# The last step of the last token block's second MLP product by whole token tiles, and two products' operands made ahead in the other blocks

## The chip, the cores and the metric

The kernel runs on one core of a Trainium2 chip. Its engines take their instructions in a fixed order each and wait for one another by semaphores: TensorE (PE) for matmuls, VectorE (DVE), ScalarE (ACT), GpSimd (POOL), and the queues of transfers, most of which SyncE (SP) issues. The metric is the time of one launch on the device, in microseconds; of several runs the median counts. Nearly all work in the kernel is in float32.

## The reference

One step of a hybrid decoder layer, on a new prompt of 2,048 tokens and on 64 sample tokens (8 sequences of 8 tokens, with 8,192 cached tokens each). Attention with forgetting and a matrix-memory branch are mixed, projected, added to the input and normalized; then comes the MLP, which the change is about:

```python
x1 = _layer_norm(DN_ALPHA * x + mix, ln1_g, ln1_b)
hid = jnp.square(jax.nn.relu(x1 @ w1))
return _layer_norm(DN_ALPHA * x1 + hid @ w2, ln2_g, ln2_b)
```

`x1` has 1,024 columns, `hid` 4,096. The prompt's rows go to `y_prompt`, the sample's to `y_sample`.

## The kernel before

**Phases.** Earlier phases project the input, attend over the prompt and run the matrix memory. The sample tokens' attention over the cache runs beside everything else: its pieces (`attend`) are put between other work by a pace (`tick`), read cached keys and values by gathers, and go on into the MLP phase. The MLP, `phase_c` (L1262), comes last.

**Blocks and steps.** Tokens stand in tiles of 128, 0 to 15 for the prompt; tile 16 holds the 64 sample tokens. `CB` makes four blocks of them, 0 to 3; the last has 12, 13, 14, 15 and 16 (576 tokens), the others four tiles (512). In each block the 4,096 hidden units are taken in eight steps `p` of 512. `hidden(p, half)` (L1325) makes 256 of them from x1 and `w1` in PSUM tiles `ph`, and ACT squares the positive part into `hq`. `output(p, ...)` (L1412) multiplies the step's 512 hidden units with 512 rows of `w2` and adds into the rows `y`. The loop at the end of the phase does the first half of the next step's hidden units, then this step's output, then the other half.

**Products in three parts.** PE multiplies float32 exactly enough only by halves: an operand is split by ACT into a rounded high part (`split_hi`, L154) and by DVE into the rest (`split_lo`, L157), and `mm3` (L162 to L165) does high x high, high x low and low x high. `hh` and `hl` are the parts of hidden units, `wh` and `wl` those of weights, `x1h` and `x1l` those of x1. The sample tile's output is multiplied without a split, in `two_sides` (L168 to L170), for two halves of the hidden units side by side.

**Strassen's products.** For one step and four tiles, the second product is a 2 x 2 block product: token tiles in two pairs, hidden units in two halves, columns of `w2` in two halves. `output` does it by Strassen's method with seven products in place of eight: sums of hidden blocks are made by DVE in `made` (L1392 is the sum's helper), sums of blocks of weights were made in earlier phases and lie in `dw2`, and each product's PSUM tiles are added to several rows of y by `add` (L1355, its instruction L1362). A product is 12 matmuls of 128x512; a step has 84. The order is 1, 5, 6, 3, 7, 2, 4 in blocks 0 to 2 and 1, 2, 5, 3, 6, 7, 4 in block 3. `operands` and `made` load, sum and split for a product; they run three products ahead of PE in program order, and `ahead(p, ...)` makes the first ones before `output` begins: the first two of the order in steps 0 to 6, product 1 alone in step 7.

**Weights.** In blocks 0 to 2 they are loaded into five buffers `wr` that the first product's weights use too; in block 3 into the six places of a ring (`kT`, `spare`) that the sample attention has left. `wh` and `wl` have four buffers each, `hh` and `hl` three.

**What stands around step 7.** In blocks 0 to 2 step 7 also turns the next block's x1: PE transposes a tile (`px`, L1171), and ACT and DVE split it into `x1h` and `x1l`; the next block's first product needs all of them. In block 2 the hidden stage before step 7 does the sample tokens' output projection and first norm (`sampled`, L1294 to L1316; instructions on L1310, L1311, L1315, and `norm_quick`, L187 to L198), since tile 16 belongs to block 3. `C["normed"]`, the norm's last DVE instruction on L197, is put ahead of everything that `output` of that step issues, by `issue_after`; what `ahead` has made is outside of this.

**The end.** In block 3 `add` counts the additions to each half row (`due`). When a half is complete its statistics are taken (L1370), and when both are, `norm_quick` norms the tile and sends it out: L189 and L191 on DVE, a power on POOL (L192), two instructions each on L195 and L197 on DVE, two transfers (L198).

**Order.** The instructions of each engine are put in a fixed order when the program is built, by a scheduler that follows the dependences and the `issue_after` orders; so an edit can move instructions that it does not name.

Of the kernel before, what the change touches and what calls it, by code (L numbers as in the profile page):

```python
# [52 lines left out]
def body(ctx, tc, I, O, stages):  # L53
# [841 lines left out]
    def phase_b():  # L895
# [173 lines left out]
        for n in range(len(units) + LA):  # L1069
            if 10 <= n < 16 and acc[1] is not None:  # L1070
                attend()
            w2_due[0] += 64 * (n % 8 // 2 + 1) / 130 if n >= 8 else 0
            while n and len(w2_done) < min(64, w2_due[0]):
                w2_sum()
            if n == 60:
                wo.extend(half_wo(0, q) for q in range(4))
            if n < len(units):
                h, g = units[n]
                sc[n] = scores(Z[h], g)
                if h == 0 and g % 2 == 0 and g < 6:  # L1080
                    keys(Z[0], g // 2 + 1)
                if h < 7:
                    if g == 3:
                        Z[h + 1] = head(h + 1)
                        forget_values(Z[h + 1], 0, S)
                    if g >= 4:
                        keys(Z[h + 1], g - 4)
                if n + 1 < len(units):
                    queries(Z[units[n + 1][0]], units[n + 1][1])
            if n >= LA:  # L1090
                h, g = units[n - LA]
                values(Z[h], g, sc.pop(n - LA))
# [183 lines left out]
    def phase_c():  # L1276
# [5 lines left out]
        def vecs(l):  # L1282
            g = bcast(I[f"ln{l}_g"], 0, D, f"g{l}", pcw, tag="wr", bufs=5)
            b = bcast(I[f"ln{l}_b"], 0, D, f"b{l}", pcw, tag="wr", bufs=5)
            return g, b
# [42 lines left out]
        for ci, blk in enumerate(CB):  # L1328
# [28 lines left out]
            def add(t, half, ps, op=OP.add):  # L1357
                n = tok_n(t)
                y = ys[t][:n, half * 512:half * 512 + 512]
                due[t, half] = due.get((t, half), 0) + 1  # L1360
                if (t, half) in seen:
                    V.tensor_tensor(y, y, ps, op=op)  # L1362
                else:
                    seen.add((t, half))
                    V.scalar_tensor_tensor(y, y, ALPHA, ps, op0=OP.mult, op1=op)
                if ci == 3 and due[t, half] == 8 * sums[blk.index(t) // 2, half]:
                    first_ = t not in stats
                    if first_:
                        stats[t] = pc.tile([128, 2, 6], F32, name="ln_s2", bufs=5)
                    V.bn_stats(stats[t][:n, half], y)  # L1370
                    if not first_:
                        norm_quick(ys[t][:n], n, stats.pop(t), *C["gb"], pc, y_out(t))

            def operands(p):

                f1, f2 = H.pop((p, 0)), H.pop((p, 1))
                a11, a21, a12, a22 = f1[:, :, 0:256], f1[:, :, 256:512], f2[:, :, 0:256], f2[:, :, 256:512]
                s = ph.tile([128, 2, 256], F32, name="s", bufs=1)

                def split(x):  # L1380
                    h = ph.tile([128, 2, 256], F32R, name="hh", bufs=3)
                    l = ph.tile([128, 2, 256], F32R, name="hl", bufs=3)
                    split_hi(h, x)
                    split_lo(l, x, h)
                    return h, l

                def w(src):
                    wr = (spare() if W > 512 else raw()).rearrange("p (k c) -> p k c", k=2)
                    SY.dma_start(wr, src.rearrange("p (k c) -> p k c", k=2))
                    return (*piece(None, wr), wr)  # L1390

                v = lambda o, x, y, op: V.tensor_tensor(o, x, y, op=op)  # L1392

                def made(n):
                    if n == 1:
                        r = split(a11), w(I["w2"][p, 0])
                        v(s, a21, a22, OP.subtract)
                        v(a21, a11, a21, OP.subtract)
                        v(a11, s, a11, OP.subtract)
                    elif n == 5:  # L1400
                        r = split(s), w(dw2[p, 0])
                        v(s, a12, a11, OP.add)
                    else:
                        r = {6: lambda: (split(a11), w(dw2[p, 2])), 3: lambda: (split(s), w(I["w2"][p, 3])),
                             7: lambda: (split(a21), w(dw2[p, 1])), 2: lambda: (split(a12), w(I["w2"][p, 2])),
                             4: lambda: (split(a22), w(dw2[p, 3]))}[n]()
                    return r

                hs = [f[:, :, 512:576] for f in (f1, f2)] if W > 512 else []
                return made, hs  # L1410
# [3 lines left out]
            def output(p, ahead, begun=None):  # L1414
# [12 lines left out]
                extra = {2: (1, ((0, 0, ADD), (0, 1, SUB), (1, 0, ADD))), 3: (5, ((0, 1, ADD), (1, 1, ADD)))}  # L1427
                for at_, n in enumerate(order):
                    kind, first_, last_, r0, half, op = plan[n]
                    if p == 7 and at_ == 2 and ci == 3:  # L1430
                        C["gb"] = vecs(2)
                    for m in order[:at_ + 3]:
                        if m not in ops:
                            ops[m] = made(m)
# [26 lines left out]
                if begun:  # L1461
                    for hf in range(2):
                        turn(ci + 1, 4, hf, begun)

            def y_out(t):
                return O["y_sample"].rearrange("b t d -> (b t) d") if t == 16 else O["y_prompt"][0, t * 128:(t + 1) * 128]

# [6 lines left out]
            def ahead(p, *ns):  # L1474
                made, hs = operands(p)
                r = made, hs, {}
                for n in ns:
                    r[2][n] = made(n)
                return r
# [2 lines left out]
            hidden(0, 1)  # L1482
            for p in range(8):
                pre = []
                if p < 7:
                    hidden(p + 1, 0, lambda: pre.append(ahead(p, *order[:2])))
                else:
                    pre.append(ahead(p, 1))
                if p == 6:
                    vx["more"] = None  # L1490
                with ExitStack() as es_:
                    if "normed" in C:
                        es_.enter_context(tc.issue_after(C.pop("normed").ins))
                    output(p, pre[0], begun if p == 7 and ci < 3 else None)
                if p == 7 and ci < 3:
                    vx["more"] = landing
                    C["w1"] = w1_pieces(0)
                    C["gb"] = vecs(2)
                    later = [normed(t, ys[t], C["gb"]) for t in blk]
                if p == 6 and ci < 3:  # L1500
                    take_back()
                    begun = [x1_load(t) for t in CB[ci + 1][:2]]
                if p == 6 and ci == 2:
                    while acc[1] is not None:
                        tick(100.0)
                if p < 7:
                    hidden(p + 1, 1, sampled if p == 6 and ci == 2 else None)
        es.close()

    wo = []  # L1510
# [434 lines left out]
```

## Time and profile before

| what | value |
|---|---|
| median of 3 runs (lowest, highest) | 3236.75 us (3231.51, 3241.11) |
| profiled execution | 3245.35 us |
| its span, first to last instruction | 3242.4 us |
| mean granted clock of PE | 0.987 |
| start of the MLP blocks 0, 1, 2, 3 | 1568.65, 1984.77, 2412.1, 2827.38 us |
| output of step 7 in block 2 | 2780.7 to 2827.4 us |
| output of step 7 in block 3, to the last instruction of DVE | 3195.9 to 3238.87 us |

The profile is of one execution. The page begins with each engine's busy time and its share of the span; a window is a stretch of the span with the same numbers. In a timeline each row has the start, the duration, the engine, the line of the kernel and the operation with the tile that it writes and those that it reads; `x16` says that a row stands for 16 instructions of one kind in a row, and a bracket at the end of a row is the engine's idle time before it and what ended it. A duration includes the part in which the next instruction of the engine has already begun, so prices are read from one start to the next. The view of the waits adds up such idle times by pairs: who waited for whom, in all, how often, and the longest.

### The profile page before, as it was taken

What the parts mean: (1) busy time and instruction counts of PE and PEld (TensorE: products, weight loads), DVE (VectorE), ACT (ScalarE), POOL (GpSimd) and SP (SyncE); (2) the same over time, 40 slices, a digit from 0 to 9 for tenths busy, and PEclk for the clock granted to TensorE, in tenths of its full rate; (3) what the DMA queues carried; (4) which work ended last, traced back from release to release, by engine and by line L of the source; (5) the groups of instructions that cost most, each with busy time, mean ns of one, the idle gap of its engine ahead of it and who ended that gap; (6) DMA issues with size and microseconds to landing.
All of it is one profiled execution on the core that took longest, in us unless ns stands there. A gap on an engine that the chain in (4) does not pass through costs nothing. (4 is left out here: it accounts for less than half of the span.)

```text
span 3242.4 us, 57713 instructions
## 1 busy us (share of the span) xinstructions
PE 3127.7 (96%) x21585; PEld 2535.8 (78%) x21585; DVE 2095.6 (65%) x5062; ACT 1489.0 (46%) x2940; POOL 907.2 (28%) x974
## 2 busy tenths in 40 slices
PE   8899999999989999999999999999999999899997
PEld 8898998998956666677677777776777777698895
DVE  6866657456478788544466568656586665766658
ACT  3342343343378888522344345343454444344442
POOL 0021233323334333276233423433333121000000
PEclk9999999999989999999999999999999999999999
DMA  5465776866667776487887878868779766543322
GB/s 188 128 220 174 254 225 202 277 238 232 228 220 204 185 181 150 171 300 262 294 291 277 296 270 308 317 243 328 289 282 338 279 212 210 208 147 137 121 95 81
DMA packets 339775, 734.34 MB, mean 226 GB/s; under 512 B 63656, under 2 KB 177704, under 8 KB 338600
## 3 DMA queue, kind: packets, MB, share of 16 engines
q1 hardware_dynamic: 252360, 416.18, 39.2%
q0 software_dynamic: 83520, 304.12, 26.7%
q10 hardware_dynamic: 3616, 10.36, 0.9%
q8 instruction: 170, 2.79, 0.3%
q14 instruction: 109, 0.89, 0.1%
HBM read 677.71 MB, written 86.38 MB: 236 GB/s over the span
## 5 line engine op out<-in xcount | busy, mean ns | idle before, releaser
L157 DVE TENSOR_TENSOR wl<-wr,wh 128x1024 fp32r<-128x1024 f32 x300 | 366.0, 1222 | 249.5 <-ACT wh L154 241.9
L163 PE MATMUL ph<-x1h,wh 128*128 128x512 f32 (+1 forms) x1280 | 455.2, 356 | 0.0
L164 PE MATMUL ph<-x1l,wh 128*128 128x512 f32 (+1 forms) x1280 | 453.0, 354 | 0.2 <-DVE x1l L157 0.2
L165 PE MATMUL ph<-x1h,wl 128*128 128x512 f32 (+1 forms) x1280 | 450.5, 354 | 0.7 <-DVE wl L157 0.4
L154 ACT ACTIVATE wh<-wr 128x1024 fp32r<-128x1024 f32 x300 | 315.4, 1053 | 290.1 <-PE ph L164 162.4
L1662 POOL DMA_INDIRECT kT<-cache_k,idxK x256 | 275.8, 1077 | 540.7 <-PE sQ L1685 477.2
L163 PE MATMUL py<-wh,hh 128*128 128x512 f32 x896 | 358.3, 403 | 6.4 <-ACT hh L154 3.7
L164 PE MATMUL py<-wl,hh 128*128 128x512 f32 x896 | 352.4, 395 | 5.5 <-DVE wl L157 5.5
L165 PE MATMUL py<-wh,hl 128*128 128x512 f32 x896 | 349.2, 395 | 2.1 <-DVE hl L157 2.1
L1362 DVE TENSOR_TENSOR y<-y,py 128x512 f32<-128x512 f32 x416 | 281.5, 682 | 98.9 <-PE py L165 94.8
L163 PE MATMUL pm<-xh,whi 128*128 128x256 f32 (+1 forms) x1024 | 299.5, 292 | 0.0
L164 PE MATMUL pm<-xl,whi 128*128 128x256 f32 (+1 forms) x1024 | 295.5, 289 | 0.0
L165 PE MATMUL pm<-xh,wlo 128*128 128x256 f32 (+1 forms) x1024 | 294.5, 288 | 0.0
L1773 POOL DMA_INDIRECT vt<-cache_v,idxV x164 | 177.7, 1084 | 384.3 <-PE sO L1797 316.9
L163 PEld LDWEIGHTS ph<-x1h,wh 128*128 128x128 f32 x1280 | 241.2, 188 | 40.8 <-issue 7.8
L165 PEld LDWEIGHTS ph<-x1h,wl 128*128 128x128 f32 x1280 | 240.3, 188 | 37.1 <-issue 3.7
L164 PEld LDWEIGHTS ph<-x1l,wh 128*128 128x128 f32 x1280 | 241.2, 188 | 34.4 <-issue 3.3
L163 PE MATMUL pm<-whi,xh 128*128 128x256 f32 (+2 forms) x816 | 238.1, 292 | 9.4 <-ACT whi L154 8.4
L164 PE MATMUL pm<-wlo,xh 128*128 128x256 f32 (+2 forms) x816 | 233.8, 287 | 0.6 <-DVE wlo L157 0.6
L165 PE MATMUL pm<-whi,xl 128*128 128x256 f32 (+2 forms) x816 | 233.4, 286 | 0.0
L163 PEld LDWEIGHTS py<-wh,hh 128*128 128x128 f32 x896 | 169.0, 189 | 60.4 <-issue 14.5
L1003 ACT ACTIVATE S<-S,mx 128x512 f32<-128x512 f32 (+2 forms) x320 | 207.7, 652 | 18.4 <-DVE mx L989 17.1
(363 smaller groups left out, 6829.1 us busy)
## 6 DMA issues: line engine op xcount, KB each, us to landing
wr<-w SPq DMA_DIRECT2D x200, 512.0 KB
wra<-w_in SPq DMA_DIRECT2D x104, 512.0 KB
wr<-dw SPq DMA_DIRECT2D x96, 512.0 KB
dw<-w POOLq DMA_DIRECT2D x48, 512.0 KB, 8.1
Rb<-dR SPq DMA_DIRECT2D x128, 128.0 KB
kT<-dw SPq DMA_DIRECT2D x32, 512.0 KB
kT<-w SPq DMA_DIRECT2D x24, 512.0 KB
xn<-xp_t SPq DMA_DIRECT2D x16, 512.0 KB
```

What stands on the lines that cost most here:

```text
L154: last["ACT"] = A.activation(dst, src, AF.Copy, scale=scale)
L157: r = (eng or V).tensor_tensor(dst, src, hi.bitcast(F32), op=OP.subtract)
L163: T.matmul(ps, wh, xh, start=first, stop=False, skip_group_check=shared)
L164: T.matmul(ps, wh, xl, start=False, stop=False, skip_group_check=shared)
L165: last["PE"] = T.matmul(ps, wl, xh, start=False, stop=stop, skip_group_check=shared)
L1003: last["ACT"] = A.activation(sp[:, :w], sp[:, :w], AF.Exp, bias=mx[:, 7:8], accum_out=lp[:, k:k + 1])
L1362: V.tensor_tensor(y, y, ps, op=op)
L1662: G.indirect_dma_start(out=piece(n), out_offset=None, in_=ck, in_offset=IO(ap=idxK[:, b, j // 2, j % 2:j % 2 + 1], axis=0))
L1773: vx["last"] = G.indirect_dma_start(out=vt.rearrange("p f c -> p (f c)"), out_offset=None, in_=cv, in_offset=IO(ap=idxV[:, b, (kt % 4) * 4 ...
```

## The change

In block 3 step 7 is done by a new function, `plain`, without sums: for each of the tiles 12 to 15 and each half of the columns, four pairs of hidden units and weights into one PSUM tile, 12 matmuls, eight such groups, 96 matmuls in all; then one `add`. The weights are four blocks of `w2` itself. Blocks 0 and 2 are loaded and split by `early`, which `hidden(7, 1)` calls between its two halves, 1 and 3 in `plain`. The fourth low half of hidden units uses the buffer of `s`, which is free without sums. `hh` gets a fourth buffer, in all steps. The sample tile's four half sums come from the same eight matmuls of `two_sides`, two to a PSUM tile for one half of the columns. The last addition that starts a row's statistics is counted anew. In step 7 of blocks 0 to 2 `ahead` makes products 1 and 5, not 1 alone.

```diff
--- before.py
+++ after.py
@@ -1070,7 +1070,7 @@
             if 10 <= n < 16 and acc[1] is not None:
                 attend()
             w2_due[0] += 64 * (n % 8 // 2 + 1) / 130 if n >= 8 else 0
-            while n and len(w2_done) < min(64, w2_due[0]):
+            while n and len(w2_done) < min(60 if False else 64, w2_due[0]):
                 w2_sum()
             if n == 60:
                 wo.extend(half_wo(0, q) for q in range(4))
@@ -1363,7 +1363,7 @@
                 else:
                     seen.add((t, half))
                     V.scalar_tensor_tensor(y, y, ALPHA, ps, op0=OP.mult, op1=op)
-                if ci == 3 and due[t, half] == 8 * sums[blk.index(t) // 2, half]:
+                if ci == 3 and due[t, half] == 7 * sums[blk.index(t) // 2, half] + (2 if t == 16 else 1):
                     first_ = t not in stats
                     if first_:
                         stats[t] = pc.tile([128, 2, 6], F32, name="ln_s2", bufs=5)
@@ -1378,7 +1378,7 @@
                 s = ph.tile([128, 2, 256], F32, name="s", bufs=1)
 
                 def split(x):
-                    h = ph.tile([128, 2, 256], F32R, name="hh", bufs=3)
+                    h = ph.tile([128, 2, 256], F32R, name="hh", bufs=4)
                     l = ph.tile([128, 2, 256], F32R, name="hl", bufs=3)
                     split_hi(h, x)
                     split_lo(l, x, h)
@@ -1427,8 +1427,6 @@
                 extra = {2: (1, ((0, 0, ADD), (0, 1, SUB), (1, 0, ADD))), 3: (5, ((0, 1, ADD), (1, 1, ADD)))}
                 for at_, n in enumerate(order):
                     kind, first_, last_, r0, half, op = plan[n]
-                    if p == 7 and at_ == 2 and ci == 3:
-                        C["gb"] = vecs(2)
                     for m in order[:at_ + 3]:
                         if m not in ops:
                             ops[m] = made(m)
@@ -1462,6 +1460,56 @@
                     for hf in range(2):
                         turn(ci + 1, 4, hf, begun)
 
+            def weight(src):
+                wr = spare().rearrange("p (k c) -> p k c", k=2)
+                SY.dma_start(wr, src.rearrange("p (k c) -> p k c", k=2))
+                return (*piece(None, wr), wr)
+
+            lastw = {}
+
+            def plain(p):
+
+                f = H.pop((p, 0)), H.pop((p, 1))
+                C["gb"] = vecs(2)
+                x = {}
+
+                def part(r, n):
+                    h = ph.tile([128, 2, 256], F32R, name="hh", bufs=4)
+                    if len(x) < 3:
+                        l = ph.tile([128, 2, 256], F32R, name="hl", bufs=3)
+                    else:
+                        l = ph.tile([128, 2, 256], F32R, name="hl4", tag="s", bufs=1)
+                    a = f[n][:, :, r * 256:r * 256 + 256]
+                    split_hi(h, a)
+                    split_lo(l, a, h)
+                    x[r, n] = h, l
+
+                for n in range(2):
+                    part(0, n)
+                for q in (1, 3):
+                    lastw[q] = weight(I["w2"][p, q])
+                for n in range(2):
+                    part(1, n)
+                for half in range(2):
+                    ps = ppc.tile([128, 512], F32, name="ph", tag="ph", bufs=2)
+                    for k in range(2):
+                        two_sides(ps, [(f[n][:, k, 512:576], lastw[n * 2 + half][2][:, k]) for n in range(2)], k == 0, k == 1)
+                    for n in range(2):
+                        add(16, half, ps[n * 64:n * 64 + 64])
+                for i in range(4):
+                    r, c = i // 2, slice(i % 2 * 128, i % 2 * 128 + 128)
+                    for half in range(2):
+                        ps = ppc.tile([128, 512], F32, name="py", bufs=4)
+                        for n in range(2):
+                            (h, l), (wh, wl, _) = x[r, n], lastw[n * 2 + half]
+                            for k in range(2):
+                                mm3(ps, h[:, k, c], l[:, k, c], wh[:, k], wl[:, k], n == k == 0, n == k == 1, True)
+                        add(blk[i], half, ps)
+
+            def early():
+                for q in (0, 2):
+                    lastw[q] = weight(I["w2"][7, q])
+
             def y_out(t):
                 return O["y_sample"].rearrange("b t d -> (b t) d") if t == 16 else O["y_prompt"][0, t * 128:(t + 1) * 128]
 
@@ -1482,10 +1530,13 @@
             hidden(0, 1)
             for p in range(8):
                 pre = []
+                if p == 7 and ci == 3:
+                    plain(p)
+                    break
                 if p < 7:
                     hidden(p + 1, 0, lambda: pre.append(ahead(p, *order[:2])))
                 else:
-                    pre.append(ahead(p, 1))
+                    pre.append(ahead(p, *order[:2]))
                 if p == 6:
                     vx["more"] = None
                 with ExitStack() as es_:
@@ -1504,7 +1555,7 @@
                     while acc[1] is not None:
                         tick(100.0)
                 if p < 7:
-                    hidden(p + 1, 1, sampled if p == 6 and ci == 2 else None)
+                    hidden(p + 1, 1, {2: sampled, 3: early}.get(ci) if p == 6 else None)
         es.close()
 
     wo = []
```

The orders below are of the built programs, without times. The numbers tell buffers apart. First DVE in block 2's step 7, from the first sum of hidden blocks: y_30222 is the sample tile, s_30317 a sum that is product 5's operand, wr_30337 product 5's weights, wr_30348 those of product 6. Before:

```order
L1392 TENSOR_TENSOR s_30317<-hq_29890,hq_30188 128x512
L1392 TENSOR_TENSOR hq_29890<-hq_29890 128x2x256
L1392 TENSOR_TENSOR hq_29890<-s_30317,hq_29890 128x2x256
L189 BN_AGGR ln_m2_30279<-ln_s2_30237 64x2
L191 TENSOR_SCALAR ln_r2_30281<-ln_m2_30279 64x1
L195 SCALAR_TENSOR_TENSOR y_30222<-y_30222,ln_m2_30279,g1_30216 64x512 x2
L197 SCALAR_TENSOR_TENSOR y_30222<-y_30222,ln_r2_30281,b1_30218 64x512 x2
L157 TENSOR_TENSOR hl_30334<-s_30317,hh_30333 128x512
L157 TENSOR_TENSOR wl_30340<-wr_30337,wh_30339 128x1024
L157 TENSOR_TENSOR hl_30345<-hq_29890,hh_30344 128x512
L157 TENSOR_TENSOR wl_30351<-wr_30348,wh_30350 128x1024
```

With the change, from the weights of product 5 (here wr_30335), which are split beside the sample attention's own work (L1868) and ahead of the projection (L1310):

```order
L157 TENSOR_TENSOR wl_30338<-wr_30335,wh_30337 128x1024
L1868 TENSOR_REDUCE mixs_2655<-sT_30164 64x8 x8
L1310 SCALAR_TENSOR_TENSOR y_30222<-y_30222,py_30224 64x256
...
L1392 TENSOR_TENSOR s_30317<-hq_29890,hq_30188 128x512
L157 TENSOR_TENSOR hl_30332<-s_30317,hh_30331 128x512
L1392 TENSOR_TENSOR s_30317<-hq_30188,hq_29890 128x512
L195 SCALAR_TENSOR_TENSOR y_30222<-y_30222,ln_m2_30279,g1_30216 64x512 x2
L197 SCALAR_TENSOR_TENSOR y_30222<-y_30222,ln_r2_30281,b1_30218 64x512 x2
L157 TENSOR_TENSOR hl_30345<-hq_29890,hh_30344 128x512
L157 TENSOR_TENSOR wl_30351<-wr_30348,wh_30350 128x1024
```

The low half of product 5's operand (hl_30332) and the third sum now stand ahead of the norm; the weights of product 5 are gone from the stretch; product 6's operand and weights (hl_30345, wl_30351) still follow the norm.

PE with the change, from its leaving the hidden stage of block 3's last step; ph_33925 and ph_33934 are the sample tile's sums for the two halves of the columns, py_33953 is tile 12's first half, py_33969 its second, py_33995 tile 13's first:

```order
L170 MATMUL ph_33925<-kT_11264,hq_33468 64x512
L170 MATMUL ph_33925<-kT_11264,hq_33776 64x512
L163 MATMUL py_33953<-wh_33832,hh_33899 128x512
...
L165 MATMUL py_33953<-wh_33837,hl_33904 128x512
L163 MATMUL py_33969<-wh_33908,hh_33899 128x512
L163 MATMUL py_33995<-wh_33832,hh_33899 128x512
...
L164 MATMUL py_33995<-wl_33833,hh_33899 128x512
L170 MATMUL ph_33934<-kT_11264,hq_33468 64x512
L170 MATMUL ph_33925<-kT_11264,hq_33776 64x512
L170 MATMUL ph_33934<-kT_11264,hq_33776 64x512
L164 MATMUL py_33969<-wl_33909,hh_33899 128x512
```

Where before a whole product of Strassen's came first and the sample tile's eight matmuls in one piece after 24 matmuls, three of the eight now come first and five after 18 matmuls of whole tiles.

DVE at the very end. y_31015 to y_31021 are tiles 12 to 15. Before:

```order
L1370 BN_STATS ln_s2_34097<-y_31019 128x6
L1370 BN_STATS ln_s2_34106<-y_31021 128x6
L1362 TENSOR_TENSOR y_31019<-y_31019,py_33898 128x512
L191 TENSOR_SCALAR ln_r2_34081<-ln_m2_34079 128x1
L195 SCALAR_TENSOR_TENSOR y_31017<-y_31017,ln_m2_34079,g2_33972 128x512 x2
L197 SCALAR_TENSOR_TENSOR y_31015<-y_31015,ln_r2_34062,b2_33974 128x512
L1362 TENSOR_TENSOR y_31021<-y_31021,py_33899 128x512
L197 SCALAR_TENSOR_TENSOR y_31015<-y_31015,ln_r2_34062,b2_33974 128x512
L1370 BN_STATS ln_s2_34097<-y_31019 128x6
L197 SCALAR_TENSOR_TENSOR y_31017<-y_31017,ln_r2_34081,b2_33974 128x512 x2
L1370 BN_STATS ln_s2_34106<-y_31021 128x6
L189 BN_AGGR ln_m2_34116<-ln_s2_34097 128x2
```

With the change:

```order
L1362 TENSOR_TENSOR y_31021<-y_31021,py_34079 128x512
L191 TENSOR_SCALAR ln_r2_34028<-ln_m2_34026 128x1
L195 SCALAR_TENSOR_TENSOR y_31017<-y_31017,ln_m2_34026,g2_33895 128x512 x2
L189 BN_AGGR ln_m2_34068<-ln_s2_34051 128x2
L1370 BN_STATS ln_s2_34093<-y_31021 128x6
L197 SCALAR_TENSOR_TENSOR y_31017<-y_31017,ln_r2_34028,b2_33897 128x512
L1362 TENSOR_TENSOR y_31021<-y_31021,py_34095 128x512
L197 SCALAR_TENSOR_TENSOR y_31017<-y_31017,ln_r2_34028,b2_33897 128x512
L191 TENSOR_SCALAR ln_r2_34070<-ln_m2_34068 128x1
L195 SCALAR_TENSOR_TENSOR y_31019<-y_31019,ln_m2_34068,g2_33895 128x512 x2
L1370 BN_STATS ln_s2_34093<-y_31021 128x6
L197 SCALAR_TENSOR_TENSOR y_31019<-y_31019,ln_r2_34070,b2_33897 128x512 x2
```

Before, the last additions of tiles 14 and 15 came close together after two products, and two norms followed them; now the tiles come one after another, and after the last addition tile 14 still has most of its norm ahead and tile 15 all of it.

## The prediction

> **What bounds the kernel now.** I read the page first, then busy time by windows cut at the borders of the stages, then the waits and the order of time in the two windows where TensorE (PE) is not full. The page's first part, and four windows (borders; length, busy time and count on PE, weight loads, DVE, ACT, POOL; granted clock; DMA share; GB/s):
>
> ```profile
> PE 3127.7 (96%) x21585; PEld 2535.8 (78%) x21585; DVE 2095.6 (65%) x5062; ACT 1489.0 (46%) x2940; POOL 907.2 (28%) x974
> 3000.00:3195.00 195.00, 194.86 (x1171) 169.01 (x1171) 128.15 (x165) 87.27 (x137) 0.00 (x0) 1.00 0.30 108
> 2774.50:2793.00 18.50, 18.37 (x113) 12.76 (x112) 4.14 (x16) 5.44 (x8) 0.00 (x0) 1.00 0.56 195
> 2793.25:2827.19 33.94, 23.61 (x104) 18.21 (x104) 33.84 (x53) 14.49 (x20) 1.00 (x1) 0.85 0.67 227
> 3205.88:3238.87 32.99, 14.28 (x58) 10.09 (x56) 32.86 (x61) 3.25 (x5) 5.41 (x5) 0.86 0.16 56
> ```
>
> Over the whole span, and in four steps of block 3 (3000 to 3195), the bound is PE: 194.86 of 195.00 us, with DVE a third idle. The two places that the change edits most are different. In block 2's last step DVE is busy 33.84 of 33.94 us while PE is short of work by 10 us; in the last 33 us of the kernel DVE is busy 32.86 of 32.99 us and PE less than half. So in both places time is saved by taking work from DVE (or starting it sooner), and twelve matmuls more on PE can be free. Just before block 2's last step (2774.5 to 2793) DVE is idle for 14 of 18.5 us: there is room to do something sooner.
>
> The end, in order of time (start, duration, engine, line, operation; a bracket is an idle time before and what ended it):
>
> ```profile
> 3195.91 0.39 PE L163 MATMUL py<-wh,hh 128*128 128x512 f32 x1
> 3201.46 3.65 PE L170 MATMUL ph<-kT,hq 128*64 128x512 f32 x16
> 3222.68 0.39 PE L164 MATMUL py<-wl,hh 128*128 128x512 f32 x1
> 3224.95 0.39 PE L165 MATMUL py<-wh,hl 128*128 128x512 f32 x1
> 3225.53 1.27 DVE L1370 BATCH_NORM_STATS2 ln_s<-y 128x6 f32<-128x512 f32 x2
> 3226.73 0.66 DVE L1362 TENSOR_TENSOR y<-y,py 128x512 f32<-128x512 f32 x1
> 3227.32 0.13 DVE L191 TENSOR_SCALAR ln_r<-ln_m 128x1 f32<-128x1 f32 x1
> 3233.14 0.32 DVE L189 BATCH_NORM_AGGREGATE ln_m<-ln_s 128x2 f32<-128x12 f32 x2
> 3236.14 2.73 DVE L197 SCALAR_TENSOR_TENSOR y<-y,ln_r,b 128x512 f32<-128x512 f32 x4
> ```
>
> PE is done at 3225.34, DVE at 3238.87; the last output transfer ends with the span, 3242.4, which is 3.5 us later and stays so, since the same transfer follows the same last instruction. From starts to starts come the prices: a statistics instruction and an add of a 128x512 tile 0.60 us each (3225.53, 3226.73, 3227.32), two whole norms of a tile 3238.87 - 3233.14 = 5.73, so 2.86 each, a back-to-back matmul (3224.95 - 3222.68)/10 = 0.227.
>
> **The change part by part: the last step of block 3.** It goes from 84 to 96 matmuls of three-fold split products; the eight of the sample tile on L170 (3.65 us) stay. On DVE it removes four sums of hidden blocks (L1392), three low halves of operands (hl), three low halves of weights (wl), six adds of 128 rows (14 to 8) and one of the sample tile (5 to 4); statistics (10) and norms (5) stay.
>
> ```profile
> 3198.80 0.69 DVE L1392 TENSOR_TENSOR s<-hq 128x512 f32<-128x512 f32 x1
> 3199.41 0.68 DVE L1362 TENSOR_TENSOR y<-y,py 128x512 f32<-128x512 f32 x1
> 2799.05 0.67 DVE L157 TENSOR_TENSOR hl<-s,hh 128x512 fp32r<-128x512 f32 x1
> 2799.65 1.21 DVE L157 TENSOR_TENSOR wl<-wr,wh 128x1024 fp32r<-128x1024 f32 x1
> 2800.78 0.67 DVE L157 TENSOR_TENSOR hl<-hq,hh 128x512 fp32r<-128x512 f32 x1
> ```
>
> A sum is 0.61 us (3198.80 to 3199.41), hl 0.60, wl 1.13. Removed: 4 x 0.61 + 3 x 0.60 + 3 x 1.13 + 7 x 0.60 = 11.8 us. If DVE stayed full from the same point this would be the gain, and it is the upper bound. It does not quite, as the new order leaves DVE idle once. By the order of the change, PE runs three L170, 12 matmuls of tile 12, six more, then the other five L170: 3195.91 + 3 x 0.456 + 18 x 0.227 + 5 x 0.456 = 3203.6, and with 0.3 us until DVE sees it the sample's second sum is there at 3203.9. All splits of operands and weights are done by then (they begin inside the hidden stage, where DVE is a third idle, and the last of them need about 4 us after 3195.9), and DVE waits. What it has left at 3203.9: two sample adds, 10 statistics, 7 adds, 19 x 0.60 = 11.4, and five norms, 14.3; together 25.7, and the end at 3229.6 in place of 3238.87: **-9.3 us**. The same from PE: 96 x 0.227 + 3.65 after 3195.91 is 3221.4 if PE never waits, then 0.3, the last two adds and statistics with two norms, 2 x 1.2 + 5.7, to 3229.8. Both agree; I take -9.3. The lower bound is a PE that keeps the waits that it has in this step now:
>
> ```profile
> PE py L163 <- DVE y L1362: 2.6, 2, 1.7
> PE py L163 <- ACT hh L154: 1.7, 1, 1.7
> PE py L165 <- DVE hl L157: 0.9, 1, 0.9
> ```
>
> These are 5.2 us, so PE's way would end at 3229.8 + 5.2 = 3235.0 and the gain be 3.9. The new step has eight groups on four PSUM buffers, the fifth following an add that came nearly 10 us before, so the first kind should go; the second and third are splits, and these are early now. The three weight loads of 512 KB that go from SP's queue cost nothing either way, with the DMA share at 0.16.
>
> **The early weights and the fourth hh buffer.** Two loads and their splits, 2 x 1.13 us on DVE and the like on ACT, move into block 3's last hidden stage. There PE is full and DVE has 67 of 195 us free, ACT more: cost 0. Without this cover they would be 2.3 us of DVE. The fourth hh buffer lets ACT run ahead in steps where PE misses 0.14 of 195 us: 0. The edit that reads 64 with either branch changes no number.
>
> **Two products' operands ahead in blocks 0 to 2.** Nothing is added; instructions change places. The last step of block 2:
>
> ```profile
> 2793.25 0.68 DVE L1392 TENSOR_TENSOR s<-hq 128x512 f32<-128x512 f32 x1
> 2794.64 0.73 PE L163 MATMUL py<-wh,hh 128*128 128x512 f32 x2 [1.77 <-ACT hh L154]
> 2796.40 1.40 DVE L195 SCALAR_TENSOR_TENSOR y<-y,ln_m,g 64x512 f32<-64x512 f32 x2
> 2797.72 1.40 DVE L197 SCALAR_TENSOR_TENSOR y<-y,ln_r,b 64x512 f32<-64x512 f32 x2
> 2800.91 0.80 PE L164 MATMUL py<-wl,hh 128*128 128x512 f32 x1 [5.54 <-DVE wl L157]
> 2826.92 0.53 PE L1171 MATMUL px<-ident,xr 64*128 64x64 f32 x4 [1.33 <-DVE x1l L157]
> 2827.38 0.61 PE L163 MATMUL ph<-x1h,wh 128*128 128x288 f32 x1
> ```
>
> PE waits 5.54 us for product 5's wl, which stands on DVE behind the sample tile's norm. The change puts that wl ahead of the norm, into DVE's idle stretch. PE's long wait then mostly moves: product 6's hl and wl still stand behind the norm, now 1.2 us later in it, and after 24 matmuls PE stands until about 2802. What ends the stage is DVE: from 2793.25 to the last x1l, on which the next block's first product (2827.38) waits, DVE is full, and what is left between these two is one wl less, 8 to 7. So **-1.1 us**. Bounds: 0 if the piece is lost again to a wait of DVE for PE, and if PE's waits set the end, all of 5.54 + 1.77 and the half clock behind them, which is in this window (same columns):
>
> ```profile
> 2796.45:2806.69 10.24, 5.78 (x14) 4.52 (x15) 10.21 (x15) 2.50 (x3) 1.00 (x1) 0.50 0.76 255
> ```
>
> Its 14 matmuls at 0.5 lose 14 x 0.2 = 2.8 us: -10.1 in all. I stay near the end to which the full DVE points. In blocks 0 and 1 the operand of product 5 is by the order of the change no earlier on DVE than it was, and there the whole of block 1 and 2's steps shows this:
>
> ```profile
> PE sO L1797 <- DMA vt<-cache_v,idxV: 7.4, 3, 2.8
> PE py L165 <- DVE hl L157: 1.0, 1, 1.0
> PE px L1171 <- DVE x1l L157: 0.5, 1, 0.5
> ```
>
> Between -1.5 (both operand waits gone) and one more wait of the first kind; I take 0. **The sum:** -9.3 - 1.1 = -10.4, from the profiled 3245.35 us (span 3242.4 and 2.95 around it) to 3234.95. That execution lies 8.6 above the median of the runs shown, 3236.75, from which I subtract the same: 3226.35, rounded 3226.
>
> **The rivals.** *PE goes on waiting in the last step* (buffers, or a split that is late): 3.9 + 1.1 = -5.0, 3232. For it: every wait there now is of this kind. Against: none of the three has its cause left. *In block 2 PE, not DVE, was the bound*: -9.3 - 10.1 = -19.4, 3217. For it: 5.54 us with a half clock in one place. Against: DVE's 33.84 of 33.94. *Slower: the cached keys and values of the sample attention.* Its matmuls stand between blocks 1 and 2's steps, fed by gathers; the change shifts their places in PE's order by up to 16 matmuls, 3.65 us, and one that comes too early stops PE, with everything behind it:
>
> ```profile
> 2406.04 1.07 PE L1797 MATMUL sO<-vt,PTs 128*32 128x256 f32 x16 [2.78 <-DMA vt<-cache_v,idxV]
> 2408.15 0.63 PE L163 MATMUL py<-wh,hh 128*128 128x512 f32 x1
> 2410.28 0.61 PE L165 MATMUL py<-wh,hl 128*128 128x512 f32 x1
> ```
>
> The price is here: 2.78, then half speed, (2410.28 - 2408.15)/5 = 0.426 for each of eight matmuls, 1.6 more: 4.4 us. Three new ones (13.2) outweigh the gain, five (22) make 3236.75 - 10.4 + 22 = 3248, slower beyond doubt. For it: three such waits stand in blocks 1 and 2 now, so the margin is thin. Against: shifts go both ways, and the longest is hardly above one wait. The Trainium skill (TensorE: Matmul & The Clock Gate, Part 1, What's actually happening) says that the clock falls to half only after at least one idle window of about 3.4 us, free-running: by that a wait of 2.78 would cost itself alone, five cost 14, and the result be 3240. The trace does not side with it: the 2.78 was followed by half speed. *The change does not do what it says* in blocks 0 and 1; that is in the sum already.
>
> **How the numbers follow.** The forecast has a chance of 0.55, with a range of its own from 3221 to 3231 (the -1.5 of blocks 0 and 1, half of block 2's bound, or half of the lost waits); PE still waiting 0.19; block 2 wholly freed 0.18; attention waits 0.08. The range that leaves out 2 in 10 is 3216 to 3235. A measurement of this kernel tells about 0.3% from no change, 9.7 us, so faster means below 3227.0. The forecast is only just below: of its 0.55 I give 0.36 to faster and 0.18 to same, 0.01 to slower; the freed block 2 is all faster; PE waiting is 0.17 same, 0.02 faster; attention is 0.06 slower, 0.01 same and 0.01 faster. Faster 0.57, same 0.36, slower 0.07.
>
> **What would show it.** Right: PE from its leaving the hidden stage to its end about 25.5 us with under 1 us of waits; DVE idle some 3 us before about 3204 and then full for 25.7; in block 2's last step PE's wait for wl near 4 us and behind product 5, DVE full, the step 1.1 us shorter. Wrong: a PE wait on an add of y or on wl in the last step; PE less than full between 3000 and 3195; block 2's step shorter by over 3 us; other waits on vt or kT in blocks 1 and 2, or a different start of block 3 that block 2's last step does not explain.

## The result and the profile after

| | before | with the change |
|---|---|---|
| median of 22 runs | 3239.33 us | 3232.31 us |
| lowest, highest | 3229.76, 3250.42 | 3220.88, 3246.08 |
| ratio, 95% interval | | 0.9975 [0.9964, 0.9986] |
| profiled execution, its span | 3245.35, 3242.4 | 3233.31, 3231.3 |

The change makes the kernel faster by 0.25%, which is 8.1 us of 3239, between 4.5 and 11.7 (the medians themselves differ by 7.0). Forecast were 10.4. The interval ends below 1, so the kernel is faster; but it lies on both sides of the 0.3% that the prediction asked for before it would say faster, and 0.25% is below that.

Windows of the changed kernel's trace in the columns used above: four steps of block 3, its last hidden stage, the DVE stretch of block 2's last step (from the first sum of hidden blocks to the last low half of the next x1), and the last step of block 3 in two parts.

```profile
3000.00:3185.00 185.00, 184.87 (x1100) 159.26 (x1099) 122.28 (x159) 81.43 (x126) 0.00 (x0) 1.00 0.31 106
3178.00:3192.68 14.68, 14.68 (x95) 13.50 (x93) 6.67 (x10) 6.82 (x12) 0.00 (x0) 1.00 0.00 1
2791.71:2824.42 32.71, 23.85 (x103) 18.29 (x103) 32.65 (x52) 13.45 (x19) 1.00 (x1) 0.89 0.67 220
3192.68:3201.67 8.99, 8.99 (x36) 4.63 (x35) 5.08 (x6) 2.41 (x4) 0.00 (x0) 1.00 0.00 0
3201.67:3227.79 26.12, 17.89 (x78) 14.46 (x78) 25.73 (x49) 0.00 (x0) 5.15 (x5) 0.92 0.21 71
```

PE is still full in the steps of block 3, and in the last hidden stage, where the early weights now lie. The DVE stretch of block 2 is still full and 1.24 us shorter (32.71 for 33.95). The last step divides at 3201.67, when the sample tile's second sum arrives: for 8.99 us PE is full and DVE is not, then DVE is full for 26.12 us. Together 35.11 us from PE's leaving the hidden stage to DVE's last instruction; before they were 3238.87 - 3195.91 = 42.96. Over the whole step DVE's busy time went from 42.46 to 30.80 us, 11.66 less, where 11.8 were counted; its idle time went from 0.50 to 4.31 us, nearly all of it in the first part.

The timeline of the changed kernel's last step, PE first, then DVE:

```profile
3192.68 1.93 PE L170 MATMUL ph<-kT,hq 128*64 128x512 f32 x6
3194.54 0.50 PE L163 MATMUL py<-wh,hh 128*128 128x512 f32 x1
...
3198.84 2.80 PE L170 MATMUL ph<-kT,hq 128*64 128x512 f32 x10
3201.57 0.50 PE L164 MATMUL py<-wl,hh 128*128 128x512 f32 x1
...
3219.17 0.39 PE L165 MATMUL py<-wh,hl 128*128 128x512 f32 x1
3197.59 0.69 DVE L1362 TENSOR_TENSOR y<-y,py 128x512 f32<-128x512 f32 x1 [1.71 <-PE py L165]
3199.99 1.40 DVE L1362 TENSOR_TENSOR y<-y,ph 64x512 f32<-64x512 f32 x2 [1.72 <-PE ph L170]
3201.67 0.68 DVE L1362 TENSOR_TENSOR y<-y,ph 64x512 f32<-64x512 f32 x1 [0.28 <-PE ph L170]
...
3226.38 1.41 DVE L197 SCALAR_TENSOR_TENSOR y<-y,ln_r,b 128x512 f32<-128x512 f32 x2
```

No PE row of this step has a wait; the three waits of before are gone, as the forecast had it. What it had too small is the sample tile's eight matmuls (two rows each here): in two pieces they take 1.86 and 2.73 us (3192.68 to 3194.54, 3198.84 to 3201.57), 4.59, where one piece took 3.59 before (3201.46 to 3205.05).

PE in block 2's step 7:

```profile
2793.10 0.50 PE L163 MATMUL py<-wh,hh 128*128 128x512 f32 x1 [1.77 <-ACT hh L154]
...
2801.27 0.77 PE L163 MATMUL py<-wh,hh 128*128 128x512 f32 x1 [4.47 <-DVE y L1362]
2801.84 0.63 PE L164 MATMUL py<-wl,hh 128*128 128x512 f32 x1
...
2824.14 0.69 PE L1171 MATMUL px<-ident,xr 64*128 64x64 f32 x4 [1.33 <-DVE x1l L157]
```

The long wait has moved behind product 5 and is 4.47 us, at half speed after it as before (0.43 from start to start). It is put down to an add of y and not to product 6's weights; that add frees the PSUM buffer, and on DVE it stands behind the norm and those weights all the same.

**The spans are not the effect.** The two profiled spans differ by 11.1 us, and this splits by block (from the first matmul of a block's first product to that of the next; the last column as above). The start lies ahead of everything that the change moves on PE.

| kernel | start of block 0 | block 0 | block 1 | block 2 | block 3 up to the last step | last step |
|---|---|---|---|---|---|---|
| before | 1568.65 | 416.12 | 427.35 | 415.26 | 368.53 | 42.96 |
| change | 1562.53 | 420.24 | 427.79 | 414.20 | 367.92 | 35.11 |

6.1 us of the difference were there when the MLP began, 4.1 were lost again in block 0. Over the 14 profiles of this study block 0 starts between 1549.86 and 1568.65 with the same program ahead of it. A single span therefore tells little here; the last step and the DVE stretch, which wait for no transfer, come back to 0.02 us in every kernel that has them unchanged, and on these the verdicts below rest.

### The profile page after: what moved, and what is told of

It is laid out like the page before. It is cut to its first block, busy times and chain, and to the rows that moved or that the text cites. A ratio compares the mean times of both kernels' runs of the same rounds, so it can differ in the third digit from the quotient of the medians.

```text
span 3231.3 us, 57635 instructions
## 1 busy us (share of the span) xinstructions
PE 3133.2 (97%) x21597; PEld 2538.1 (79%) x21597; DVE 2080.6 (64%) x5045; ACT 1483.7 (46%) x2934; POOL 915.4 (28%) x974
## 5 line engine op out<-in xcount | busy, mean ns | idle before, releaser
L163 PE MATMUL py<-wh,hh 128*128 128x512 f32 x900 | 358.0, 402 | 11.7 <-DVE y L1362 4.7
L1003 ACT ACTIVATE S<-S,mx 128x512 f32<-128x512 f32 (+2 forms) x320 | 207.8, 653 | 16.5 <-DVE mx L989 15.2
```

The source lines that it names most:

```text
L163: T.matmul(ps, wh, xh, start=first, stop=False, skip_group_check=shared)
L1003: last["ACT"] = A.activation(sp[:, :w], sp[:, :w], AF.Exp, bias=mx[:, 7:8], accum_out=lp[:, k:k + 1])
```

## The experiments

**The parts apart.** The change with product 1 alone ahead in step 7:

```diff
-                    pre.append(ahead(p, *order[:2]))
+                    pre.append(ahead(p, 1))
```

> The change without its part in blocks 0 to 2: product 1 alone is made ahead there, as before; the last step of block 3 is the new one. My theory (the time of the last step is DVE's work there, that of block 2's last step too, and the two parts add up): the last step, from PE's leaving the hidden stage to DVE's last instruction, 35 us as in the changed kernel (43 before); block 2, from its first product to that of block 3, 415.3 us as before (414.2 in the changed kernel); time 7.9 us less than before, ratio 0.9976. Rival (the gain of the change comes from the operands made ahead): a ratio of 1.000. Rival (moved sample attention costs about 4 us in block 0 of the changed kernel): block 0 is back at 416 us, from 420, and the ratio is nearer to 0.9963.

Ratio 0.9971 [0.9957, 0.9986]; last step 35.11, DVE stretch 33.96, block 2 416.88 where 415.3 was expected, block 0 417.64. The other part alone, in the kernel before:

```diff
-                    pre.append(ahead(p, 1))
+                    pre.append(ahead(p, *order[:1 if ci == 3 else 2]))
```

> The other part alone: two products' operands ahead in step 7 of blocks 0 to 2, the last step of block 3 by Strassen's sums, three hh buffers. My theory: the last step 43 us as before, block 2 1.1 us shorter than before (414.2 for 415.3), PE's long wait in its step 7 about 4.5 us and not 5.5, time 1.1 us less, which these rounds can't tell from none (ratio 0.9997). Rival (PE, not DVE, bounds block 2's step 7): block 2 shorter by 5 to 10 us. Rival (moved sample attention): block 0 about 420 us again, not 416, and the ratio above 1.000.

Ratio 0.9985 [0.9968, 1.0001]; last step 42.95, DVE stretch 32.70, the long wait 4.47, block 2 414.99, block 0 416.19. In their stages the parts add up to the hundredth: 7.85 us belong to the last step, 1.25 to block 2's stretch, and neither knows of the other. Block 2 as a whole shows it less sharply, since the rest of it scatters: over the 14 profiles it took 416.3 us in the mean with one product ahead, 415.7 with two and 414.4 with three, single ones between 414.15 and 417.68. Block 0's 420.24 us did not come back, though the first of these two kernels is built like the changed one up to block 2's last step; and the kernel before, in its other profile below, took 419.60 there. So this was scatter. The rival that PE's waits bound block 2 falls: 1.25 us, not 5 to 10.

```diff
-                    h = ph.tile([128, 2, 256], F32R, name="hh", bufs=3)
+                    h = ph.tile([128, 2, 256], F32R, name="hh", bufs=4)
```

> The kernel before with four hh buffers in place of three, nothing else. My theory: nothing, each block and the last step within 1 us of before apart from the sample attention's waits; ratio 1.000. Rival (the fourth buffer lets the split run ahead, and part of the gain of the change is this): block 3 up to the last step shorter than 367.9 to 368.5 us, or the wait of 1.67 us for hh in the last step gone and the step shorter.

Ratio 0.9994 [0.9978, 1.0009]; block 3 up to the last step 368.16, the last step 42.96, block 2 416.80 with its DVE stretch at 33.96 as before. The fourth buffer by itself is worth nothing that these runs can see.

**What sets the end.** The eight matmuls of the sample tile in one piece, behind tile 12's first half (`group` is the body of the loop over tiles, `sample` that of the sample tile):

```diff
+                group(0, 0)
+                with tc.issue_after(last["PE"].ins):
+                    sample()
+                with tc.issue_after(last["PE"].ins):
+                    for i in range(4):
+                        for half in range(2):
+                            if i or half:
+                                group(i, half)
```

> The changed kernel with PE's order in the last step held: tile 12's first half, then the sample tile's eight matmuls in one piece, then the rest. In the changed kernel they came as three and five and took 1.86 + 2.73 = 4.6 us for 3.6 in one piece before, and DVE stood idle until 9.0 us after PE had left the hidden stage, waiting for the sample tile's second sum. My theory (DVE's work from that sum on sets the end): the second sum is there at 6.5 us, DVE is full from there for 26, and the last step takes 32.5 us, 2.5 less than in the changed kernel (35.1); ratio to before 0.9968. Rival (PE's end plus what follows the last add sets it): 1.0 less, 34.1. Rival (the order has no say): 35.1.

Ratio 0.9951 [0.9932, 0.9970]. The last step of this kernel, PE and then DVE:

```profile
3195.70 0.39 PE L163 MATMUL py<-wh,hh 128*128 128x512 f32 x1
...
3198.54 3.71 PE L170 MATMUL ph<-kT,hq 128*64 128x512 f32 x16
3202.17 0.50 PE L163 MATMUL py<-wh,hh 128*128 128x512 f32 x1
3202.26 2.60 DVE L1362 TENSOR_TENSOR y<-y,ph 64x512 f32<-64x512 f32 x4 [1.73 <-PE ph L170]
...
3227.43 1.41 DVE L197 SCALAR_TENSOR_TENSOR y<-y,ln_r,b 128x512 f32<-128x512 f32 x2
```

The piece takes 3.63 us again, the sums reach DVE 6.56 us after PE's leaving, and 26.5 us of DVE follow: 33.13, 1.98 less than in the changed kernel. PE ends only 1.07 sooner (25.81 after leaving, for 26.88), so PE's end is not what counts. The 32.5 expected had taken the changed kernel's 26.1 us of DVE for the rest; here two more adds of the sample tile fall into it, and one statistics instruction less.

Two kernels that leave out work, each profiled once, then took the engines one at a time. Half of PE's:

```diff
-                        for k in range(2):
-                            mm3(ps, h[:, k, c], l[:, k, c], wh[:, k], wl[:, k], n == k == 0, n == k == 1, True)
+                        mm3(ps, h[:, 0, c], l[:, 0, c], wh[:, 0], wl[:, 0], n == 0, n == 1, True)
```

> The kernel that holds PE's order, with half of the matmuls of the four prompt tiles in the last step left out (256 of the step's 512 hidden units, so 48 of 96 matmuls and half of each sum); DVE's instructions stay. Measured with all of them: PE done 25.8 us after it leaves the hidden stage, DVE 33.1, and DVE full from the sample tile's sums (6.6) on. My theory (DVE's work sets the end): the sums are there at about 5.2, DVE has 26.5 left, and the step still takes 31.7 us though PE is done at 15. Rival (PE's end and what follows the last add): 33.1 - 10.9 = 22.2.

PE was done 14.95 us after its leaving, DVE at 31.90 (31.7 and 22.2 expected by the two):

```profile
3176.29:3208.19 31.90, 14.95 (x66) 9.99 (x64) 30.35 (x55) 2.46 (x5) 7.72 (x5) 0.82 0.16 55
```

So 10.9 us less of PE moved the end by 1.23, which is about what the sample tile's sums came sooner (5.20 us after PE's leaving, for 6.56). And less of DVE's, in `norm_quick`:

```diff
-        for i in range(2):
+        for i in range(2 if out.shape[0] == 64 else 0):
             V.scalar_tensor_tensor(x[:, h[i]], x[:, h[i]], mv[:np_, 0:1], g[:np_, h[i]], op0=OP.subtract, op1=OP.mult)
```

> The same kernel with the norm's first pair of instructions (less the mean, times gamma, L195 of before) left out for the four prompt tiles: eight instructions of 0.66 us less on DVE, PE's work unchanged. My theory: 5.3 us less work moves the end by that until PE becomes the bound. DVE alone would give 33.1 - 5.3 = 27.8; PE's end at 25.8 with 0.3, the last add and statistics (1.2), the two small instructions and POOL's power (1.5, no longer covered) and the last pair (1.4) gives 30.2; the later one holds, 30.2. Rival (the end does not depend on DVE's work): 33.1.

DVE ended at 30.64 (30.2 and 33.1 expected), 2.5 us sooner and not 5.3, and its rows now show waits for PE and for POOL's power, where the kernel with all of DVE's work has none behind the sums:

```profile
3216.72 0.69 DVE L1362 TENSOR_TENSOR y<-y,py 128x512 f32<-128x512 f32 x1 [0.69 <-PE py L165]
...
3221.64 1.41 DVE L197 SCALAR_TENSOR_TENSOR y<-y,ln_r,b 128x512 f32<-128x512 f32 x2 [0.73 <-POOL ln_r L192]
...
3225.53 1.42 DVE L197 SCALAR_TENSOR_TENSOR y<-y,ln_r,b 128x512 f32<-128x512 f32 x2 [0.73 <-POOL ln_r L192]
```

So DVE's work sets the end of the new step; of 5.3 us taken from it 2.5 came back before waits for PE and POOL took its place.

**Block 2, one product more.**

```diff
-                    pre.append(ahead(p, *order[:2]))
+                    pre.append(ahead(p, *order[:3]))
```

> The changed kernel with three products' operands made ahead in step 7 of blocks 0 to 2 (1, 5 and 6). Block 2's DVE stretch, from the first sum of hidden blocks to the last low half of the next x1, took 33.95 us with one product ahead and 32.7 with two. My theory (it is as long as DVE's work in it): product 6's weights leave it too, 1.13 us less, 31.6, and PE's long wait shrinks from 4.5 to about 2 us. Rival (PE's waits set it): as much as the wait shrinks, 30.2 or less. Rival (nothing more to gain, another wait takes its place): 32.7. Time 1 us less than the changed kernel, ratio to before 0.997 to 0.9965.

Ratio 0.9949 [0.9934, 0.9965]. The DVE stretch of this kernel:

```profile
2789.08:2820.65 31.57, 23.88 (x104) 18.36 (x104) 31.51 (x51) 13.35 (x19) 1.00 (x1) 0.89 0.66 211
```

It takes 31.57 us, another 1.14 less, the price of one wl, and is full once more (31.51). PE's long wait went from 4.47 only to 3.34, by as much as the stretch; so by their sizes shrinking the wait and shrinking DVE's work can't be told apart here. The kernel above with half of the last step's matmuls tells them apart. Up to block 3's last step it is built like the changed kernel, but in its execution PE went through product 5 partly at half speed (0.43 us from start to start, 2781.38 to 2782.24), so it came later to the long wait, which was 3.23 us and not 4.47:

```profile
2786.09 0.47 PE L163 MATMUL py<-wh,hh 128*128 128x512 f32 x1 [3.23 <-DVE y L1362]
2776.54:2809.24 32.70, 24.50 (x104) 18.04 (x104) 32.64 (x52) 13.56 (x19) 1.00 (x1) 0.90 0.67 223
```

Its DVE stretch is as long as ever with two products ahead, 32.70. So a shorter wait of PE alone gains nothing, and it is DVE's work that counts: DVE is full in all three versions (33.84 of 33.94, 32.65 of 32.71, 31.51 of 31.57) while PE stands idle for 7.7 to 10.3 us in each.

**Together, and the blocks ahead.** Both at once, by the two edits above:

> Both that helped: PE's order held in the last step and three products ahead in blocks 0 to 2. My theory: the last step 33.1 us (43.0 before), block 2's DVE stretch 31.6 (33.95 before); together 12.2 us, ratio to before 0.9962, if nothing else moves. Rival (what is gained in the steps is lost to waits of the sample attention): ratio 0.9975 or more with blocks 0 and 1 longer than 416 to 428.

Ratio 0.9963 [0.9950, 0.9976]; last step 33.13, DVE stretch 31.58, as expected; blocks 0 and 1 took 418.66 and 427.30. Each half of it alone had read a lower ratio, 0.9951 and 0.9949, lower also than was expected of them. So ratios from 5 or 6 runs of a kernel do not rank kernels that differ by a few us; the stages do. With PE's order held and three products ahead in block 2 alone:

```diff
-                    pre.append(ahead(p, *order[:2]))
+                    pre.append(ahead(p, *order[:3 if ci == 2 else 1]))
```

> PE's order held in the last step, and three products ahead in block 2 alone; blocks 0 and 1 as before. In the profiles so far blocks 0 and 1 together took 843.4, 844.4 and 842.7 us with one product ahead there, and 842.8 to 848.6, in the mean 846.4, over the seven with two or three: some 2.8 us lost to waits of the sample attention. My theory (the shifted attention costs this, and a block left alone doesn't pay it): blocks 0 and 1 together 843.5 +- 1, block 2's DVE stretch 31.6, the last step 33.1; 12.2 us less than before, ratio 0.9962. Rival (those 2.8 us are the scatter of single profiles): blocks 0 and 1 anywhere from 843 to 849.

Median 3223.76 us, ratio 0.9949 [0.9929, 0.9970]; last step 33.13, stretch 31.57; blocks 0 and 1 together 845.1. Then two products ahead in blocks 0 and 1 only, profiled twice, and the kernel before once more:

```diff
-                    pre.append(ahead(p, 1))
+                    pre.append(ahead(p, *order[:2 if ci < 2 else 1]))
```

> The kernel before with two products ahead in step 7 of blocks 0 and 1 alone. My theory (the shifted attention costs about 2.8 us there and nothing is gained): blocks 0 and 1 together 846 +- 2.5 us, with more attention waits in block 1; ratio 1.0009, not told from 1 by the clock alone. Rival (scatter): 843.5. Rival (the wait for hl in block 1 is gone and this is a gain): 842 or less.

> The same kernel as the one with two products ahead in blocks 0 and 1 alone, for a second profile. My theory: blocks 0 and 1 together 846 +- 2.5 us. Rival (scatter): 843.5 +- 1, as with one ahead.

> The kernel before, for one more profile. My theory: blocks 0 and 1 together 843.5 +- 1. Rival (scatter of single profiles): outside of 842 to 845.

Ratio 0.9998 [0.9982, 1.0013] for the kernel that asks for it in blocks 0 and 1 only.

But these edits on `ahead` change nothing in blocks 0 and 1, so the expectations above rest on a difference that isn't there. In step 7 `output` follows `ahead` at once, and before all else it makes the first three products, as far as `ahead` hasn't; whichever of the two does it, the calls come in the same order. Only in block 2 something stands between them, the `issue_after` of the sample tile's norm. Built, the kernel with two products ahead in blocks 0 and 1 is the kernel before, instruction for instruction, with the same buffers and the same waits, and its traces have the 21585 rows of PE and the 5062 of DVE in the same order. The kernel with three products ahead in block 2 alone is, in the same way, the one above with three in blocks 0 to 2. What differs in blocks 0 and 1 among the kernels of this study is only the fourth hh buffer: with it PE's order differs from the one before from within block 0 on. Blocks 0 and 1 together, in us, of all profiles, by what was built there:

| hh buffers | profiles | mean |
|---|---|---|
| three | 843.5, 847.0, 845.7, 846.7, 847.8 | 846.1 |
| four | 848.0, 844.4, 842.8, 845.0, 842.9, 848.6, 847.0, 846.0, 845.1 | 845.5 |

The difference is 0.6 us with a standard error of about 1.0. In the first row 843.5, 845.7, 846.7 and 847.8 are executions of one program, the kernel before, and lie 4.3 us apart; 847.8, its repeat, fell outside of what was expected. So the idea that the products ahead shift the sample attention there and cost 2.8 us falls: it was scatter, and the two profiles that fell into the 846 +- 2.5 expected did so by chance. The buffer is not shown to cost or to gain anything there either.

## Why the prediction came out as it did

**The bounds** were read rightly. PE is full in block 3's steps, and in the two places where it was not, DVE's work was the measure. In block 2 the work taken from DVE came back one for one (each wl of 1.13 us brought 1.24 and 1.14); in the last step 7.85 of 11.66 us came back, as the rest became idle time ahead of the second sum. The twelve more matmuls are not on the path that ends last: 48 fewer moved the end by 1.23 us.

**The last step: 9.3 us forecast, 7.85 measured.** The mechanism held: no PE wait, DVE idle ahead of the sample tile's second sum, then full to the end. The term that was mis-sized is "3195.91 + 3 x 0.456 + 18 x 0.227 + 5 x 0.456 = 3203.6", with the sum on DVE at 3203.9, 8.0 us after PE's leaving: it came at 8.99, since the eight matmuls in pieces of three and five cost 4.59 us and not 8 x 0.456 = 3.65. (The 18 matmuls between took 4.30 and not 4.09, and DVE saw the sum 0.10 us later and not the 0.3 for which the prediction gives no row; these two cancel.) That is 1.0 of the 1.45; the rest is the gaps in DVE's list, which took 26.1 us with 25.73 of it busy, where 25.7 were forecast. The other way to the same number, PE's end "with two norms" behind it, agreed by chance: PE took 26.88 us and not 25.4, and with half of its work gone the end moved by 1.2 us.

**Block 2: 1.1 forecast, 1.24 measured**, by one wl less, with the moved wait at 4.47 where "near 4" stood. **Blocks 0 and 1: 0 forecast**, and 0 from this part, for a simpler reason than the one given: there it moves no instruction at all. So the bounds given for it, from -1.5 to one more wait, had no cause. What shifts the places of the sample attention there is the fourth buffer, which the prediction put at nothing; the profiles show no loss by it (0.6 us, standard error 1.0). **The early weights and the fourth buffer: 0 forecast**, and 367.92 us for 368.53 in block 3, 368.16 with the buffer alone: nothing beyond the scatter (366.6 to 369.3 over all profiles).

**The sum.** 7.85 + 1.24 = 9.1 us by the stages, against 8.1 [4.5, 11.7] by the runs. The forecast was 1.3 above the first and 2.3 above the second. The median of 3232.31 lies 6 above the 3226 forecast, also because the kernel before has a median of 3239.33 over more runs, and not the 3236.75 from which the sum was taken. It lies just outside of the forecast's own range, 3221 to 3231, and inside of the wide one.

**The rivals.** PE went on waiting in the last step: no, no wait at all; that this rival's 3232 is the measured median is chance. Block 2 wholly freed: no, by three versions. Attention waits that make it slower: not seen at that size in any of the profiles.

**A version that does better.** One piece for the sample tile and three products ahead (in block 2 alone or in blocks 0 to 2, which is the same program): by stages 9.83 + 2.38 = 12.2 us less than before; by its two sets of runs 0.9963 [0.9950, 0.9976] and 0.9949 [0.9929, 0.9970], about 12.0 and 16.5 us; both intervals hold the 12.2. It is faster than the kernel before; that it beats the change is shown in the two stages, and by the runs only in the medians, since the intervals overlap.

## What to carry to other kernels

Look for the stretches where the busiest engine of the whole is not full: there a method that saves its work at the cost of another's (here Strassen's sums) can be the wrong one, and the work of the engine that is full there is the price of every edit. When a tail is costed by instruction counts, follow the order in which pieces reach the bounding engine too, since the time of the first late piece counted as much as the counts. Before reading a difference between two kernels, see whether their built programs differ at that place at all; here an edit of one call changed one block of three. Where gathers or other transfers scatter the whole by more than an edit is worth, judge it by the stages that repeat to hundredths, and use many runs for the total.

## What the runs showed of the hardware

Matmuls of 128x64 weights with float32 operands, two sides going to the two halves of one PSUM tile, took 1.86 us for three, 2.73 for five and 3.63 for eight (in the program's count). Taken as pairs, with a lone one counting as a pair, these are 2, 3 and 4 times 0.91 to 0.93. The rows of the changed kernel agree: each matmul has two rows, the rows of the two sides of a pair start 0.007 us apart, and the next rows come 0.43 to 0.47 us later; the two rows of a lone one stand 0.43 us apart as well (3193.59 and 3194.02). So a side without its partner costs about as much as both.

The length of a wait alone did not tell whether PE went on at half speed. In block 2's last step the changed kernel and the one with half of the last step's matmuls have the same two waits in product 5, 1.77 and 0.38 to 0.39 us; after them the first ran at 0.23 us from start to start, the second soon at 0.43.

The start of the MLP moved by 19 us among 14 executions of programs whose order on PE is the same up to there, with PE's clock between 0.987 and 0.991 in the mean over the spans of these profiles.
